# The first load of a streaming logsumexp as two transfers, of the even and of the odd partitions

## The chip, the cores and the metric

The kernel runs on one core of one Trainium2 chip. The metric is the time of the whole execution on the device in microseconds (us). The profile's span is 1.78 to 1.79 us shorter than the time of the same run. The granted clock was 1.0. ACT is ScalarE, DVE is VectorE and SP is SyncE, which here only issues transfers. In the trace of the kernel before each of the 17 loads ends with 16 completions (chunk 0's come at 6.73 to 7.40); they are read here as one for each of the core's 16 DMA engines.

## The reference

```python
def setup_inputs():
    batch, seq, dim = 32, 512, 1024
    return {"x": np.random.randn(batch, seq, dim).astype(np.float32), "axis": -1}

def reference(x, axis):
    x_max = np.max(x, axis=axis, keepdims=True)
    return (x_max.squeeze(axis) + np.log(np.sum(np.exp(x - x_max), axis=axis))).astype(np.float32)
```

There are 16,384 rows of 1,024 floats, 67.1 MB in and 64 KB out. Each of the 128 partitions handles 128 rows.

## The kernel before

The input comes through a ring of 51 rows per partition in 17 loads, all issued by SP. `CHUNKS` lists how many rows a load brings, and how many of them ACT exponentiates in one instruction with the sums left to DVE. The other rows get one ACT instruction each, which also sums.

```python
CHUNKS = [
    (4, 1), (15, 11), (16, 10), (16, 15), (16, 0), (14, 0), (12, 9), (9, 5), (7, 5), (5, 4),
    (4, 3), (3, 0), (2, 2), (2, 2), (1, 0), (1, 0), (1, 0),
]
RING_ROWS = 51
FIRST_PARTS = [("sync", 0, 128)]
# ... (set-up cut)
    def load(i):
        (s, row), r = place[i], CHUNKS[i][0]
        act_wait = max(a for a, _ in busy[s : s + r])
        dve_wait = max(d for _, d in busy[s : s + r])
        if dve_wait:
            nc.sync.wait_ge(dve_done, dve_wait)
        if act_wait:
            nc.sync.wait_ge(act_done, act_wait)
        for engine, lo, hi in FIRST_PARTS if i == 0 else [("sync", 0, P)]:
            getattr(nc, engine).dma_start(
                out=ring[lo:hi, s : s + r], in_=x_v[lo:hi, row : row + r]
            ).then_inc(landed[i], 16)
# ...
    load(0)
    n_early = len(body.instructions)
# ... (the loop over the chunks: load, wait for `landed`, exp, sum)
        nc.scalar.wait_ge(landed[i], 16 * (len(FIRST_PARTS) if i == 0 else 1))
# ... (at the end, the first n_early instructions go ahead of the opening barrier)
```

The load of chunk 0 is issued before the barrier with which the engines start. Everything else comes after it.

The softmax here doesn't subtract the row's maximum and nothing guards it: scores larger than these inputs give would overflow.

## Time and profile before

| | us |
|---|---|
| time, median of 6 runs | 164.12 (164.01 to 164.53) |
| span of the profiled run | 162.2 |
| load stream: first packet, last landing | 1.08, 158.08 |
| landing of chunk 0, of chunk 4 (last of 16 engines) | 7.40, 83.67 |
| DVE, ACT busy | 72.9, 124.1 |

Landings and packet times are read from the trace's semaphore and DMA packet records, which don't name the DMA engine. Below is the timeline of the first us of the kernel before: start, duration, engine, line, operation. "SPq" is SP's sequencer issuing a load.

```profile
0.00 0.37 SPq L85 DMA_DIRECT2D ring<-in_x_dram  x1
...
0.77 1.28 ACT L103 ACT_TABLE_LOAD   x1 [0.77 <-PEq L175]
7.42 1.06 ACT L116 ACTIVATE ring<-ring 128x1024 f32<-128x1024 f32 x1 [5.37 <-DMA ring<-in_x_dram]
```

The first issue takes 0.37 us. ACT's table load starts at 0.77, when a wait for PE's sequencer ends, and SP's next issue follows at 0.78: this is the opening barrier, and the start of the table load marks it. The first exponential waits for chunk 0 until 7.42.

### The profile page before, as it was taken

The page shows a single profiled execution, that of the slowest core. Times are in us where ns is not written, and L with a number is a line of the kernel's source. Part 1 is how long each engine was busy: PE and PEld are TensorE (multiplying, and loading weights), DVE is VectorE, ACT ScalarE, POOL GpSimd, SP SyncE. Part 2 cuts the span into 40 slices and gives each one's busy share as a digit, 9 for nine tenths or more (in the row PEclk, how much of TensorE's full clock was granted, in tenths as well). Part 3 has the DMA queues.
Part 4 walks back from the last instruction along what each step waited for, and adds up shares of the span by engine and source line. Part 5 has one row for each costly group of instructions (what it writes and reads, how often), then busy time and mean ns, then how long its engine had stood idle before and what let it go on. Part 6 is the DMA issues. An engine that isn't in the chain of part 4 may idle for free.

```text
span 162.2 us, 213 instructions
## 1 busy us (share of the span) xinstructions
DVE 72.9 (45%) x11; ACT 124.1 (76%) x136; POOL 0.2 (0%) x4
## 2 busy tenths in 40 slices
DVE  0030000039960799000999900000006999799591
ACT  3180006997099971999339999999999999999993
POOL 0000000000000000000000000000000000000000
DMA  6999899969969959969988999999999999999970
GB/s 263 497 485 470 349 394 517 485 291 517 485 291 517 517 259 517 517 275 501 517 368 370 424 424 432 461 497 388 436 427 399 431 400 439 420 424 414 415 318 16
DMA packets 2593, 67.18 MB, mean 414 GB/s; under 512 B 288, under 2 KB 416, under 8 KB 800
## 3 DMA queue, kind: packets, MB, share of 16 engines
q1 hardware_dynamic: 2448, 67.11, 96.4%
q10 hardware_dynamic: 144, 0.07, 0.1%
q14 instruction: 1, 0.01, 0.0%
HBM read 67.11 MB, written 0.07 MB: 414 GB/s over the span
## 4 chain that ended last, share of the span: by engine, by line
ACT 52%; DMA 38%; DVE 7%; issue 1%
DMA ring<-in_x_dram 38%; ACT ring L128 30%; ACT ring L116 22%; DVE sums L121 7%; ACT res L93 0%
## 5 line engine op out<-in xcount | busy, mean ns | idle before, releaser
L121 DVE TENSOR_REDUCE sums<-ring 128x5 f32<-128x5120 f32 (+8 forms) x11 | 72.9, 6648 | 86.0 <-ACT ring L116 85.9
L116 ACT ACTIVATE ring<-ring 128x5120 f32<-128x5120 f32 (+8 forms) x11 | 59.3, 5394 | 29.4 <-DMA ring<-in_x_dram 29.4
L128 ACT ACTIVATE ring<-ring 128x1024 f32<-128x1024 f32 x61 | 63.4, 1041 | 5.3 <-DMA ring<-in_x_dram 5.3
L128 ACT ACTIVATION_READ_ACCUMULATOR ring<-ring 128x1 f32 x61 | 11.4, 187 | 0.0
L103 ACT ACT_TABLE_LOAD x1 | 1.3, 1283 | 0.8 <-PEq L175 0.8
L93 ACT ACTIVATE res<-sums 128x67 f32<-128x67 f32 (+1 forms) x2 | 0.5, 256 | 0.1
L175 POOL MEMSET const-bfloat16-1.0<- 128x1 bf16 x1 | 0.1, 101 | 0.0
L175 POOL MEMSET const-uint8-127<- 128x1 uint8 x1 | 0.1, 101 | 0.0
L175 POOL MEMSET const-float32-0.0<- 128x1 f32 x1 | 0.1, 98 | 0.2 <-issue 0.2
L175 POOL MEMSET const-float32-1.0<- 128x1 f32 x1 | 0.1, 98 | 0.0
## 6 DMA issues: line engine op xcount, KB each, us to landing
ring<-in_x_dram SPq DMA_DIRECT2D x1, 7680.0 KB, 24.8
ring<-in_x_dram SPq DMA_DIRECT2D x1, 7168.0 KB, 36.1
ring<-in_x_dram SPq DMA_DIRECT2D x1, 6144.0 KB, 21.6
ring<-in_x_dram SPq DMA_DIRECT2D x1, 4608.0 KB, 32.1
ring<-in_x_dram SPq DMA_DIRECT2D x2, 2048.0 KB, 26.3
ring<-in_x_dram SPq DMA_DIRECT2D x1, 3584.0 KB, 40.2
ring<-in_x_dram SPq DMA_DIRECT2D x1, 2560.0 KB, 44.4
ring<-in_x_dram SPq DMA_DIRECT2D x2, 1024.0 KB, 46.0
```

Of the source, the lines that this page charges most:

```text
L93: nc.scalar.activation(out=res[:, lo:hi], in_=sums[:, lo:hi], func=Ln).then_inc(act_done, 1)
L103: nc.scalar.preload_act_table_set("natural_log_exp_and_others")
L116: nc.scalar.activation(out=ring[:, s : s + n_dve], in_=ring[:, s : s + n_dve], func=Exp).then_inc(act_done, 1)
L121: nc.vector.reduce_sum(out=sums[:, row : row + n_dve], in_=ring[:, s : s + n_dve], axis=AX).then_inc(dve_done, 1)
L128: nc.scalar.activation(out=ring[:, s + j], in_=ring[:, s + j], func=Exp, accum_out=sums[:, row + j : row + j + 1],).then_inc(act_done, 1)
L175: nc = _bacc.Bacc("TRN2", target_bir_lowering=False, num_devices=1)
```

## The change

The first load is split in two, presumably so that the DMA engines might get their first work sooner, and by even and odd partitions rather than halves (e2 tries the halves, which cost 3.1%). Both transfers go ahead of the barrier.

```diff
-FIRST_PARTS = [("sync", 0, 128)]
+FIRST_PARTS = [(0, 2), (1, 2)]
...
-        for engine, lo, hi in FIRST_PARTS if i == 0 else [("sync", 0, P)]:
-            getattr(nc, engine).dma_start(
-                out=ring[lo:hi, s : s + r], in_=x_v[lo:hi, row : row + r]
+        for lo, step in FIRST_PARTS if i == 0 else [(0, 1)]:
+            nc.sync.dma_start(
+                out=ring[lo:P:step, s : s + r], in_=x_v[lo:P:step, row : row + r]
             ).then_inc(landed[i], 16)
```

## The prediction

> **What bounds the kernel now.** I read the page first: busy shares (part 1) and the chain that ended last (part 4).
>
> ```profile
> span 162.2 us, 213 instructions
> DVE 72.9 (45%) x11; ACT 124.1 (76%) x136; POOL 0.2 (0%) x4
> ...
> q1 hardware_dynamic: 2448, 67.11, 96.4%
> ...
> ACT 52%; DMA 38%; DVE 7%; issue 1%
> ```
>
> The input moves for 96.4% of the span, while ACT is busy for 76% and DVE for 45%. The load stream is the scarcest resource, although the chain gives 52% to ACT. To see how both fit, I read the chain in order of time:
>
> ```profile
> 0.78 24.82 DMA ring<-in_x_dram
> ...
> 25.62 9.60 ACT ring L116
> ...
> 35.24 11.90 DVE sums L121
> ...
> 47.15 36.52 DMA ring<-in_x_dram
> ...
> 83.69 10.55 ACT ring L128 x21
> ```
>
> Up to 83.67 us the chain is two transfers with a compute step of 21.5 us between them, and that step needs care. The load issued at 47.15 (chunk 4, 16 rows into a reused part of the ring) waits for the first big reduction, so the chain goes through it. But it lands only 36.52 us later, because it queues behind the loads already issued. By the semaphore records chunk 3 has wholly landed at 64.34 and chunk 4 at 83.67: 19.3 us for 8.39 MB, or 434 GB/s. So chunk 4 was issued some 17 us before its turn. The true path is the load stream from its first packet to chunk 4, and the ACT and DVE work before 83.67 has slack. From 83.69 on ACT runs to the end practically without a gap. The waits say the same:
>
> ```profile
> ACT ring L116 <- DMA ring<-in_x_dram: 29.4, 4, 14.0
> ACT ring L128 <- DMA ring<-in_x_dram: 5.3, 1, 5.3
> ```
>
> The last of these ends at 83.69. The load stream itself ends at 158.08 (last landing), 0.1 us before the last exponential starts at 158.19. Both ends of the kernel hang on the stream's start: each us by which the early stream shifts moves the end by about one us.
>
> How the stream starts, from the windows of one us:
>
> ```profile
> 0.00:1.00 1.00, 0.00 (x0) 0.23 (x1) 0.20 (x4) 1.00 0.00 0
> 1.00:2.00 1.00, 0.00 (x0) 1.00 (x1) 0.00 (x0) 1.00 0.92 262
> 2.00:3.00 1.00, 0.00 (x0) 0.06 (x1) 0.00 (x0) 1.00 0.86 360
> 3.00:4.00 1.00, 0.00 (x0) 0.00 (x0) 0.00 (x0) 1.00 1.05 442
> ```
>
> The last column is GB/s: nothing in the first us, then 262 and 360, and the full rate from 3 us on. The packet records give the detail. The first of 128 packets of 16,384 B starts at 1.08 us, 0.70 us after the issue (0.00 to 0.37) ended. The sixteen earliest starts are spread from 1.08 to 1.97. The first packets take 0.61 to 1.36 us, later ones 0.611, which is 16 x 16,384 B / 0.611 us = 429 GB/s. Chunk 0's 16 completions come at 6.73 to 7.40, and that spread of 0.67 us is still there at chunk 4 (83.00 to 83.67). An engine that starts late stays late.
>
> [...]
>
> **The change, part by part.** The listing of the instructions shows one difference: the load of 128x4096 on SP becomes two of 64x4096. ACT, DVE and POOL are the same; ACT's first wait is for 32, not 16.
>
> - Added: one DMA issue on SP ahead of the barrier, between 0.33 and 0.37 us plus a gap of about 0.05. SP reaches the barrier at about 0.95 instead of 0.55, so the barrier opens 0.4 us later. The load of chunk 1 is issued at about 1.2 instead of 0.78. Its first packet is not needed before 6.42, when chunk 0's data of the first engine is through. Cost: 0. ACT's table load (0.77 to 2.06) shifts to about 2.46, while ACT waits for data until 7.42. Cost: 0.
> - Added: 16 completion packets of 9 ns, one per engine. Cost: 0.01 us.
> - Moved: each engine's first share is four packets instead of eight. [...] The total lost at the start is (1 - 262/436) + (1 - 360/436) = 0.57 us of stream, with 436 as the rate from 7.4 to 25.6 us. This caps the gain. Against the halving: the final store, also 128 rows on 16 engines, has its first ten packets within 35 ns[...]. [...] I take about a third of the cap: a gain of 0.2 us.
> - Each engine needs 4 x 0.611 = 2.44 us for its first share, so the second transfer, issued 0.42 us after the first, is ready in time. No gap between them.
>
> Sum: 164.13 - 0.2 + 0.01 = 163.9 us[...].
>
> **The rivals.**
>
> [...] The first 2.1 MB would take 9.8 instead of 4.9 us[...]. Nothing hides this: ACT waits 29.4 us for data early on, and chunk 4 lands later by all of it. The estimate from the packet times is +4 us, 168 us, +2.4%. [...] I give the collision 0.45, and a good part of the full cost in three quarters of such cases.
>
> *Nothing at all.* [...] Then the starts stay spread over 0.9 us and the time is 164.1. For it: even the packets that start last (1.97) need 0.73 us, and all first packets end within 2.05 to 2.69 whatever their start. Against it: the third load's issue takes 0.744 us instead of 0.33, so issuing does press against something at 1.2 to 1.9 us.
>
> *A later barrier costs.* It would add 0.4 us (164.5) if the span's first work depended on it. The windows speak against that: from 2.06 to 7.42 nothing but the load runs.
>
> **Range and chances.** A gain over 2% would need 3.3 us, while at most 0.57 plus part of the 1.08 us is lost before the full rate: 0.01. Without collisions the time is 163.6 to 164.5, within 2%. With them it is 166.5 to 169, with the 2% line at 167.41. Slower by over 2% is 0.45 x 0.75 = 0.34 and I say 0.32. The median of this mixture lies at the top of the first group: 164.1. A range that holds it 8 times in 10 must reach into the second: 163.6 to 168.3.
>
> **What would show each step right or wrong.** Two issues at 0.00 and about 0.42, the barrier 0.4 us later, chunk 1's issue near 1.2: the order of issue. The sixteen first starts: within 0.5 us of the first[...]. The packets of 16,384 B: 0.611 us says no collisions[...]. Chunk 0's last completion: 7.2 in the main case, over 10.5 with collisions, and chunk 4's landing (83.67) must move by as much as chunk 0's, as must the end. If chunk 0 moves and the end doesn't, my claim that the early stream sets the end is wrong. The prediction is also wrong if the later chunks' rates change, for example because the engines' stagger at the start is different.

The main sum came to 163.94 us, given as 163.9: 164.13, less 0.2 for the shorter first share, plus 0.01 for the completions. The 0.2 us is the author's estimate, about a third of the 0.57 us that the windows show lost at the start. "The halving" is that of the spread of the sixteen first starts, 0.89 us, which would have started the last engine 0.45 us earlier; it was an assumption. So was that 64 rows would still use all 16 engines, four packets each. The rival with 9.8 us, later called the collision, is that packets of 64 rows slow each other to half their rate. The 4.9 us is eight packets of 0.611 us; the doubling was assumed. From the 4.9 us added by it, 0.7 to 0.9 us were taken off; +4 us remained.

## The result

The changed kernel takes 164.53 us (median of 6 runs, 164.28 to 164.68), the kernel before 164.12 (6 runs). The ratio is 1.0021, with a 95% interval of 1.0007 to 1.0034: some 0.34 us slower, within 2%. A ratio here is the mean time of one kernel's fast runs over that of the other's in the same rounds, so not quite the ratio of the medians quoted.

The timeline of the changed kernel:

```profile
0.00 0.55 SPq L85 DMA_DIRECT2D ring<-in_x_dram  x1
...
1.84 1.28 ACT L103 ACT_TABLE_LOAD   x1 [1.84 <-PEq L175]
7.59 1.06 ACT L116 ACTIVATE ring<-ring 128x1024 f32<-128x1024 f32 x1 [4.47 <-DMA ring<-in_x_dram]
```

The first issue, now of 64 rows, takes 0.55 us instead of 0.37, and by the records the second takes 0.58. The barrier opens 1.07 us later. Yet chunk 0 is there only 0.17 us later. The windows of one us of the changed kernel (the last column is GB/s):

```profile
core 0: us, DVE busy (x) ACT busy (x) POOL busy (x), PEclk, DMA share, GB/s
1.00:2.00 1.00, 0.00 (x0) 0.16 (x1) 0.00 (x0) 1.00 0.60 164
2.00:3.00 1.00, 0.00 (x0) 1.00 (x1) 0.00 (x0) 1.00 0.88 360
3.00:4.00 1.00, 0.00 (x0) 0.12 (x1) 0.00 (x0) 1.00 0.97 410
```

Where the kernel before moved 262 GB/s in the second us, the changed one moves 164. A window counts a packet's bytes where the packet starts, so the first window shows best that the stream starts later. The chain of the changed kernel:

```profile
1.83 24.25 DMA ring<-in_x_dram
26.09 0.02 issue
26.11 9.60 ACT ring L116
...
35.73 11.90 DVE sums L121
...
47.65 36.51 DMA ring<-in_x_dram
84.15 0.02 issue
84.18 10.56 ACT ring L128 x21
```

It is the chain of before, shifted by 0.5 us from chunk 1 on (26.11 against 25.62, 84.18 against 83.69). The waits for data of the changed kernel say the same:

```profile
ACT ring L116 <- DMA ring<-in_x_dram: 28.8, 4, 14.3
ACT ring L128 <- DMA ring<-in_x_dram: 5.3, 1, 5.3
```

ACT waits 0.6 us less in total at L116. It has been held 1.07 us longer by the barrier and then waits 0.9 us less for chunk 0 (4.47 against 5.37). Less waiting is no gain here: the wait before chunk 1 grew from 14.0 to 14.3.

What matters at the start can be read from three packet figures: when the first packet starts, when the sixteen earliest-starting packets have ended on average, and when the 16 engines have finished chunk 0 on average.

| trace | first issue | first packet starts | first 16 packets end, mean | chunk 0 landed, mean / last | chunk 4 landed, last |
|---|---|---|---|---|---|
| before | 0.37 | 1.08 | 2.40 | 7.07 / 7.40 | 83.67 |
| changed | 0.55 | 1.34 | 2.70 | 7.33 / 7.57 | 84.15 |

### The profile page after: what moved, and what is told of

It reads as the page before. It is cut to its first block, busy times and chain, and to the rows that moved or that the text cites. A ratio compares the mean times of both kernels' runs of the same rounds, so it can differ in the third digit from the quotient of the medians.

```text
span 162.7 us, 214 instructions
## 1 busy us (share of the span) xinstructions
DVE 72.9 (45%) x11; ACT 124.1 (76%) x136; POOL 0.2 (0%) x4
## 4 chain that ended last, share of the span: by engine, by line
ACT 52%; DMA 37%; DVE 7%; issue 1%
DMA ring<-in_x_dram 37%; ACT ring L128 30%; ACT ring L116 22%; DVE sums L121 7%; ACT res L93 0%
## 5 line engine op out<-in xcount | busy, mean ns | idle before, releaser
L116 ACT ACTIVATE ring<-ring 128x5120 f32<-128x5120 f32 (+8 forms) x11 | 59.3, 5394 | 28.8 <-DMA ring<-in_x_dram 28.8
```

What stands on the lines that cost most here:

```text
L116: nc.scalar.activation(out=ring[:, s : s + n_dve], in_=ring[:, s : s + n_dve], func=Exp).then_inc(act_done, 1)
```

## The experiments

**Theory A**: the 64-row shape makes the first issue longer, hence the first packet later, and the end follows. **Rival B**: the later barrier and the later issue of chunk 1 cost. **Rival C**: a second issue in the queue slows the first. What two halves cost comes on top (e2). The experiments share one loop:

```diff
-        for lo, step in FIRST_PARTS if i == 0 else [(0, 1)]:
-            nc.sync.dma_start(
-                out=ring[lo:P:step, s : s + r], in_=x_v[lo:P:step, row : row + r]
+        for engine, lo, hi, step, a, b in FIRST_PARTS if i == 0 else [("sync", 0, P, 1, 0, r)]:
+            getattr(nc, engine).dma_start(
+                out=ring[lo:hi:step, s + a : s + b], in_=x_v[lo:hi:step, row + a : row + b]
```

A part is thus (engine, first partition, end, step, first row, end row), and each experiment differs from the changed kernel in `FIRST_PARTS`, unless more is shown. All results were correct. The times in the last but one column are those of the profiled execution. The runs were made in three groups on different chips (e1 to e4; e5 to e8 and e12; e9 to e11). The kernel before had a median of 164.01 us in the first and 164.32 to 164.33 in the others, so the ratio, taken within a group, is what can be compared, and an expected time in us only to some 0.3 us.

| run | first issue | first packet | chunk 0, mean / last | chunk 4, last | that run's time | ratio to before (95%) |
|---|---|---|---|---|---|---|
| e1 rows2 | 0.36 | 1.00 | 6.92 / 7.13 | 83.43 | 163.87 | 1.0010 (0.9996 to 1.0024) |
| e2 halves | 0.55 | 1.33 | 12.07 / 12.36 | 88.44 | 169.24 | 1.0310 (1.0297 to 1.0324) |
| e3 odd late | 0.54 | 1.32 | 7.88 / 9.15 | 85.37 | 165.62 | 1.0089 (1.0076 to 1.0103) |
| e4 two queues | 0.55 | 1.34 | 13.58 / 14.49 | 84.61 | 164.97 | 1.0029 (1.0012 to 1.0045) |
| e5 late | 0.36 | 1.72 | 7.75 / 8.24 | 84.49 | 164.80 | 1.0045 (1.0032 to 1.0058) |
| e6 quarters | 0.54 | 1.33 | 7.70 / 8.13 | 84.49 | 164.95 | 1.0048 (1.0035 to 1.0060) |
| e7 odd first | 0.55 | 1.41 | 7.31 / 7.50 | 84.08 | 164.75 | 1.0022 (1.0009 to 1.0034) |
| e8 rows 1 + 3 | 0.37 | 1.00 | 6.93 / 7.24 | 83.84 | 164.44 | 1.0002 (0.9989 to 1.0016) |
| e9 mixed | 0.36 | 0.99 | 7.06 / 7.36 | 83.79 | 164.31 | 1.0008 (0.9994 to 1.0021) |
| e10 rows2, two queues | 0.37 | 1.00 | 13.95 / 14.30 | 83.80 | 164.17 | 0.9994 (0.9981 to 1.0008) |
| e11 rows2 again | 0.37 | 1.00 | 7.06 / 7.42 | 84.01 | 164.29 | 0.9998 (0.9983 to 1.0012) |
| e12 before again | 0.37 | 1.01 | 7.14 / 7.44 | 83.98 | 164.27 | 1.0009 (0.9995 to 1.0023) |

In all these traces and those of before and after, the time less chunk 4's last landing is 80.25 to 80.80 us. It is 80.25 to 80.46 except in e2, e7, e8 and e9, where the next chunk came so late that ACT waited 0.17 to 0.44 us for it. The end hangs on the stream in every one.

The ratios fall into two groups. Six runs issue a first load of 128 partitions ahead of the barrier (e1, e8 to e12, e12 being the kernel before against itself): 0.9994 to 1.0010. Six issue one of fewer partitions there (the changed kernel, e2, e3, e4, e6, e7): 1.0021 and more. Between single runs of the two groups the intervals can overlap.

### e1: two transfers by rows, of all 128 partitions

```diff
-FIRST_PARTS = [(0, 2), (1, 2)]
+FIRST_PARTS = [("sync", 0, 128, 1, 0, 2), ("sync", 0, 128, 1, 2, 4)]
```

> Two transfers ahead of the barrier, but each of all 128 partitions and two of the four rows (packets of 8,192 B). Theory A (the shape of 64 rows makes the issue slow, 0.55 us instead of 0.37, and so the first packet late): the first issue takes 0.37 us again, the first packet starts at 1.08, and the end is 164.1 to 164.2. Rival B (what costs is that there are two transfers ahead of the barrier: the barrier opens about 1 us later and chunk 1 is issued later): first packet at 1.08, yet the end is 164.4 to 164.6 as in the changed kernel. Rival C (a second issue slows the first one, whatever its shape): first issue 0.55 us, first packet 1.34.

The timeline of this kernel:

```profile
0.00 0.36 SPq L85 DMA_DIRECT2D ring<-in_x_dram  x1
```

With 128 rows the issue takes 0.36 us although a second follows, so C falls. The first packet is at 1.00. The barrier lets ACT go at 1.24, and chunk 1 is issued then, 0.46 us later than in the kernel before. The median of 164.3 lies between A's figure and B's. The ratio of 1.0010 has an interval from nothing to the full cost, so it doesn't decide between A and B. The repeat e11 gave 0.9998 and leaves B little room.

### e2: two halves

```diff
-FIRST_PARTS = [(0, 2), (1, 2)]
+FIRST_PARTS = [("sync", 0, 64, 1, 0, 4), ("sync", 64, 128, 1, 0, 4)]
```

> Two transfers of 64 partitions each, but partitions 0 to 63 and 64 to 127 (step 1). Theory A1 (64 rows are slow to issue): first issue 0.55 us as with even and odd. Theory A2 (the step of two partitions is slow to issue): first issue 0.37 us. [...]packets of 16,384 B take about 1.2 us instead of 0.611, chunk 0 lands 4 to 5 us later than 7.4, and the time is 168 to 169. [...]

The figures from the 1.2 us on are those for halves loaded at half the rate, an assumption; 1.2 us is about twice 0.611. If halves cost nothing, 164.1 to 164.6 was expected.

The windows of this kernel:

```profile
3.00:4.00 1.00, 0.00 (x0) 0.11 (x1) 0.00 (x0) 1.00 1.12 229
4.00:5.00 1.00, 0.00 (x0) 0.00 (x0) 0.00 (x0) 1.00 0.72 147
5.00:6.00 1.00, 0.00 (x0) 0.00 (x0) 0.00 (x0) 1.00 1.09 229
```

The stream runs at about half its rate (147 to 246 GB/s in the windows from 3 to 10 us, against 410 to 426 in the changed kernel's from 3 to 6), and most packets after the first two of a share take 1.26 to 1.29 us instead of 0.611. What in the chip halves the rate was not shown. Chunk 0 lands 4.96 us after the kernel before's and the end is 3.1% later, 5.1 us (a median of 169.14, just above the 168 to 169 expected): a loss at the very start passes to the end whole. With even and odd partitions (changed, e7) the median packet takes 0.611 us and 109 or 110 of the 128 at most 0.63, so nothing of this happens there. The first issue takes 0.55 us at a step of 1 too (A1): the number of rows (64, against 0.37 us with 128), not the step, makes it long.

### e3: the odd partitions behind the barrier

```diff
-FIRST_PARTS = [(0, 2), (1, 2)]
+FIRST_PARTS = [("sync", 0, 128, 2, 0, 4), ("sync", 1, 128, 2, 0, 4)]
...
-    n_early = len(body.instructions)
+    n_early = 1
```

> As changed, but only the even partitions are loaded ahead of the barrier and the odd ones behind it. Theory A: the first packet still starts at 1.34 (the issue of 64 even rows is slow by itself), and the end is 164.4 to 164.6, although the barrier opens 0.6 us earlier than in the changed kernel. Rival B (the late barrier costs): the end is back at 164.1 to 164.3. Rival C (a second issue in the queue slows the first): first issue 0.37 us.

The first issue and two windows of this kernel:

```profile
0.00 0.54 SPq L85 DMA_DIRECT2D ring<-in_x_dram  x1
...
4.00:5.00 1.00, 0.00 (x0) 0.00 (x0) 0.00 (x0) 1.00 0.79 295
5.00:6.00 1.00, 0.00 (x0) 0.00 (x0) 0.00 (x0) 1.00 0.99 393
```

The first packet starts at 1.32 and the first issue takes 0.54 us, although no second issue follows ahead of the barrier: as A has it and C doesn't. But the end was expected at 164.4 to 164.6 and came at 165.52, a miss. The odd transfer was issued at 1.18 and its issue ended at 1.66, yet between 4.5 and 5.5 only 12 to 14 of the 16 engines have a packet in flight. Some engines had presumably used up their even share and had no odd packet yet. The packets are longer too: an engine's eight of chunk 0 take 5.67 us on average, against 5.18 in the changed kernel, which is most of the 0.55 us by which chunk 0's mean landing is later. One engine ends chunk 0 at 9.15 when the mean is 7.88. Its packets, each starting where the one before ended, can be followed from there to chunk 4, where it is still 1.1 us behind the mean (85.37 against 84.27). So the split seems to put at risk that the second part is there in time. In the changed kernel, with the second issue at 0.605, at least 15 of the engines had a packet from 3 us on. Why some engines got the odd rows so late, and why the packets were longer, is open.

### e4: the odd partitions through ACT's queue

```diff
-FIRST_PARTS = [(0, 2), (1, 2)]
+FIRST_PARTS = [("sync", 0, 128, 2, 0, 4), ("scalar", 1, 128, 2, 0, 4)]
```

> Even partitions issued by SP, odd ones by ACT, both ahead of the barrier. Theory A: SP's issue still takes 0.55 us and the first packet starts at about 1.34, the barrier at about 0.9; the end is 164.3 to 164.6. Rival B: with the barrier only some 0.2 us late the end is 164.1 to 164.2.

ACT issued the odd part at 0.12 us, and it landed only at 14.49. The engines took packets of the two queues in turn (by the packet records, one of the odd part about every 2.9 us on each engine once chunk 1 was under way), so it shared them with chunk 1. That does no harm by itself: the first exponential came late, but ACT had slack until chunk 1 (14.0 us of waiting before it in the kernel before). The cost of 0.29% can't be told from the changed kernel's 0.21%. SP's issue of 0.55 us and the first packet at 1.34 are as A has them (ACT's issue of 64 rows took 0.55 us too, that of 128 rows in e10 0.38); the barrier opened at 1.47, not at the expected 0.9, so the run says little about B. In this trace more was lost in chunks 2 to 4, where packets of 65,536 B took 2.45 us on average instead of 2.42.

### e5: one load, but behind the barrier

```diff
-FIRST_PARTS = [(0, 2), (1, 2)]
+FIRST_PARTS = [("sync", 0, 128, 1, 0, 4)]
...
-    n_early = len(body.instructions)
+    n_early = 0
```

> The kernel before with its one first load moved behind the opening barrier, nothing else. It delays the stream's first packet without touching a shape. Theory A (the end follows the stream's start one to one): the first packet starts 0.4 to 0.8 us later against the first load's issue in the kernel before, and the whole time rises by the same 0.4 to 0.8 us, to 164.5 to 164.9. Rival (the slack of ACT and DVE hides a late start): 164.0 to 164.2.

The timeline of this kernel:

```profile
0.73 1.28 ACT L103 ACT_TABLE_LOAD   x1 [0.73 <-PEq L175]
0.73 0.36 SPq L85 DMA_DIRECT2D ring<-in_x_dram  x1
```

The barrier is earlier here than in the kernel before and no shape has changed; only the issue is at 0.73 instead of 0.00. The first packet starts 0.64 us later, chunk 0 lands 0.68 us later on average, and the time rises by 0.45%, 0.74 us. That is one to one within the interval (0.53 to 0.95 us). The median of 165.03 is above the 164.5 to 164.9 expected, in a group in which the kernel before took 164.32.

### e6: four quarters

```diff
-FIRST_PARTS = [(0, 2), (1, 2)]
+FIRST_PARTS = [("sync", k, 128, 4, 0, 4) for k in range(4)]
```

(The kernel that ran had the four parts written out.)

> Four transfers of every fourth partition (32 rows each), all ahead of the barrier. If an issue takes longer the fewer rows a transfer has, the first issue takes over 0.55 us, the first packet starts later than 1.34 and the end is 164.7 or more. If any shape but 128 rows costs the same 0.55, the first packet starts at 1.34 again, and four issues of 0.55 open the barrier at about 2.9 us; the end stays at 164.4 to 164.6 if the late barrier costs nothing. Each engine's share of a transfer is then two packets (1.22 us) and an issue every 0.6 us keeps ahead of it. Packets stay at 0.611.

The timeline of this kernel:

```profile
0.00 0.54 SPq L85 DMA_DIRECT2D ring<-in_x_dram  x1
```

An issue of 32 rows takes 0.54 us and the first packet is at 1.33: both as with 64. So the cost of the first issue doesn't grow as rows fall; every shape here short of 128 partitions has it. But the end at 165.02 is a miss: 164.4 to 164.6 was expected with these figures, some 0.2 us more in this group. The four parts landed on average at 3.74, 5.01, 6.43 and 7.70, steps of 1.27, 1.42 and 1.27 us, where two packets of 0.611 are 1.22 us. Chunk 0 was thus 0.37 us later than in the changed kernel. The packet records take this apart: an engine's eight packets take 5.45 us on average against 5.18, so 0.27 us is longer packets, and 0.10 us is time without a packet. From 2.1 to 2.85 us only 10 to 14 of the 16 engines have one in flight; in the changed kernel at least 15 do from 2.3 us on. Why is open.

### e7: the odd partitions first

```diff
-FIRST_PARTS = [(0, 2), (1, 2)]
+FIRST_PARTS = [("sync", 1, 128, 2, 0, 4), ("sync", 0, 128, 2, 0, 4)]
```

> The changed kernel with the odd partitions first. A repeat in all that the theories name: first issue 0.55, first packet 1.34, end 164.3 to 164.7. It shows whether chunk 1's long packets (seven of its first sixteen took 2.48 to 2.85 us instead of 2.27 in the changed kernel) come back (systematic) or not (chance): if they are part of the cost, chunk 1's last landing is again 0.5 us after the kernel before's 25.6, otherwise 0.2 to 0.3.

The same result: 1.0022, issue 0.55, chunk 0 at 7.31 on average against 7.33. The long packets at the start of chunk 1 came back, but weaker: five of the first sixteen at 2.35 to 2.71 us, against seven (2.34 to 2.85) in the changed kernel. Among chunk 1's first sixteen packets, those over 2.3 us number nine in e3 and all sixteen in e2, but none in the three traces with one load (before, e5, e12). They aren't tied to the shape alone: e4 has none there, e9 and e11 two each, and in other places such packets turn up too, in e6 at 16 us and in e8 and e12 at 20. Chunk 1 landed 0.32 us after the first trace of before, near what was expected if they are chance, so whether they belong to the change stays open.

### e8: one row, then three

```diff
-FIRST_PARTS = [(0, 2), (1, 2)]
+FIRST_PARTS = [("sync", 0, 128, 1, 0, 1), ("sync", 0, 128, 1, 1, 4)]
```

> Two transfers of all 128 partitions: one row each first (packets of 4,096 B), then three rows (12,288 B). If smaller first packets let the sixteen engines start closer together, as two rows each did (spread 0.53 instead of 0.89 us), the spread is below 0.5 us and chunk 1 lands 0.2 to 0.3 us before the kernel before's 25.6; the end 163.7 to 164.0. Rival[...]: 164.1 to 164.5.

The rival's reasons were that the small packets' own cost eats the gain (4,096 B take a median of 0.161 us, where a quarter of 0.611 is 0.153) or that the second transfer isn't ready in time.

The sixteen earliest packets started within 0.34 us, but three of them had ended by then, so they can be those of fewer than sixteen engines. Sixteen packets are in flight at once only 0.42 us after the first start; that is below 0.5 us too, as hoped. Chunk 0 landed 0.13 us earlier on average. But seven packets at 20 us took up to 2.81 us, chunk 1's last landing was 25.79, and the time is unchanged (1.0002): the end of 163.7 to 164.0 didn't come, and the rival's 164.1 to 164.5 did. Taken as the time until sixteen packets are in flight, the start's spread goes with the first packets' size where one queue is used: 0.42 us with 4,096 B, 0.49 to 0.53 with 8,192 (e1, e9, e11), 0.76 to 0.92 with 16,384 (before, changed, e2, e3, e5, e7, e12), whether the transfer has 128 rows or 64. Two runs don't fit: four quarters (e6) take 1.75 us and e10, with 8,192 B through two queues, 0.98. The reason was not tested.

### e9: two rows of all partitions, then even and odd

```diff
-FIRST_PARTS = [(0, 2), (1, 2)]
+FIRST_PARTS = [("sync", 0, 128, 1, 0, 2), ("sync", 0, 128, 2, 2, 4), ("sync", 1, 128, 2, 2, 4)]
```

> First load in three transfers ahead of the barrier: rows 0 and 1 of all 128 partitions, then rows 2 and 3 of the even and of the odd partitions. The two 64-row transfers and a barrier later than in the changed kernel (at about 2.2 us) are kept; only the very first transfer has 128 rows again. Theory A (the late first packet is what costs): first packet at 1.00, as with two rows each, end within 0.15 us of the kernel before. Rival B (the late barrier and the late issue of chunk 1) and rival D (64-row transfers anywhere ahead of the barrier cost, for instance by gaps between an engine's shares): 0.3 to 0.8 us over the kernel before.

The timeline of this kernel:

```profile
0.00 0.36 SPq L85 DMA_DIRECT2D ring<-in_x_dram  x1
...
2.24 1.28 ACT L103 ACT_TABLE_LOAD   x1 [2.24 <-PEq L175]
```

The barrier is 0.4 us later than even in the changed kernel, and both 64-row transfers are there. But the first packet is at 0.99 and chunk 0 lands at 7.06 on average, as in the kernel before. The cost is 0.08%, 0.13 us, with an interval from -0.1 to 0.34 us. A is favoured, as its figure is met; the lowest figure of B, and of D (64-row transfers anywhere ahead of the barrier cost), 0.3, lies just inside the interval. The kernel before against itself gave 1.0009 (e12), so 1.0008 can't be told from nothing. The landing of chunk 0 is the stronger evidence.

### e10: by rows, through two queues

```diff
-FIRST_PARTS = [(0, 2), (1, 2)]
+FIRST_PARTS = [("sync", 0, 128, 1, 0, 2), ("scalar", 0, 128, 1, 2, 4)]
```

> Rows 0 and 1 of all partitions issued by SP, rows 2 and 3 by ACT. If the extra 0.6 us of even on SP and odd on ACT came from the 64-row shape (late first packet), this ends with the kernel before or below (164.0 to 164.3 where that has 164.1). If it came from two queues taking turns on the engines, it costs 0.3 us or more again, and the part issued by ACT lands later than 10 us.

Both expectations met in part: ACT's part lands at 14.30, so the queues do take turns, but it costs nothing (0.9994). The two queues were not what made e4 slow.

### e11 and e12: repeats

> A repeat of two transfers of 128 partitions and two rows each, to see whether its profile (chunk 4 landed 0.24 us earlier than in the kernel before) or its first timing (ratio 1.001, 0.9996 to 1.0024) is what holds. Theory A gives 0 to 0.2 us below the kernel before; if the first packet's 0.08 us is eaten by chance stretches later, no difference.

> The kernel before once more, to see how much of two traces' difference is chance. First issue 0.37 us, first packet at 1.08, ratio 1.000. In the traces so far the last landing of chunk 4 minus the start of the first packet lies between 82.4 and 84.0 us (81.8 to 83.1 for halves and odd_late without their extra cost); if it differs from the first trace's 82.60 by 0.2 us or so, then the 0.2 us that the changed kernel lost beyond its later first packet is within chance.

e11 is the kernel of e1 once more, e12 the kernel before. The second trace of two rows each has chunk 4 at 84.01, the first 83.43. The second trace of the kernel before has it at 83.98, the first 83.67: 82.97 us after its first packet against 82.60. Two executions of one kernel thus differ by 0.3 to 0.6 us at chunk 4 by chance; long packets (two over 2.3 us at the start of chunk 1 in e11, some at 20 us in e12) may be much of it. The start varies less. Chunk 0's mean landing was 7.07 and 7.14 in the two traces of before, 7.33 and 7.31 in those of even and odd, though 6.92 and 7.06 in those of two rows each. No version tried beats the kernel before by more than its noise.

## Why the prediction was right or wrong

**What bounds the kernel: right.** The early stream sets the end, us for us. The later start in e5 and the slower first 2.1 MB in e2 came out at the end whole (0.64 to 0.68 us gave 0.74; 4.96 us gave 5.1).

**The later barrier costs nothing: right in its conclusion, wrong in its size.** The barrier came 1.07 us later rather than 0.4. The issues took 0.55 and 0.58 us rather than 0.33 to 0.37; the barrier then opened 0.65 us after the end of the second issue, where before it opened 0.40 us after the end of the first; why is open. Chunk 1's issue moved to 1.83 instead of 1.2. e9, with a still later barrier, loses 0.13 us by the best estimate, not resolved from zero.

**"Added: one DMA issue on SP": the step that failed.** It counted the new issue and took the first issue's duration from a row with 128 partitions. The first issue itself got longer, 0.55 instead of 0.37, and nothing hides that one: the first packet starts only 0.71 us after its end before, and 0.79 us after it now. The first packet came later by 0.33 us (mean of 1.34 and 1.41 against mean of 1.08 and 1.01), and chunk 0 landed 0.22 us later on average (mean of 7.33 and 7.31 against mean of 7.07 and 7.14). This 0.22 us is the part of the 0.34 us that the runs show. In the same pairs of traces chunk 1 and chunk 4 land 0.32 us later on average; the 0.1 us between is about what the longer packets of chunk 1 add (a mean of 2.290 and 2.281 us against 2.269 and 2.274, eight to an engine). Whether they belong to the change is open (e7), and 0.1 us is inside the interval (0.11 to 0.56 us) and inside what two traces of one kernel differ by.

**"Moved: each engine's first share is four packets instead of eight": failed too.** The gain of 0.2 us didn't come. The sixteen starts were spread over 0.92 us (1.34 to 2.27) instead of halving. The working assumed that the spread goes with the number of rows; the reason it gave was not shown. With one queue the spread goes with the packet's size (0.42 us at 4,096 B, 0.76 to 0.92 at 16,384 B) and is the same with 128 rows as with 64 (e8); what sets it is open. That 64 rows use all 16 engines, as the prediction assumed, held: each of the two parts brought 16 landings spread over 0.5 us, and 16 packets were in flight at once.

**Collisions: the rival didn't happen.** The packets of 16,384 B kept to a median of 0.611 us. That packets of 64 rows can slow to about half their rate shows in e2 (1.26 to 1.29 us), where it cost 5.1 us, though not why; the estimate of 4 us for a doubling was in the right region. The chance of 0.45 given to it is what stretched the range up to 168.3.

**The number: inside the range, partly by luck.** The measured 164.53 lies inside 163.6 to 168.3, just above the group without collisions (163.6 to 164.5). The median of 164.1 equals the figure of "nothing at all" only because it is the middle of a mixture with collisions. The main sum of 163.9 had the sign wrong. The nearest figure is the 164.5 of "a later barrier costs", and that is chance: it stood for 0.4 us from the barrier, which the runs don't support, while the longer first issue is in none of the rivals.

## What to carry to other kernels

When the load stream sets the end from its first byte, the first issue is on the critical path, while the later ones here had slack as long as they came in time (e9, with chunk 1 issued behind a barrier at 2.24, has a ratio of 1.0008; e3's odd part was late, 1.0089): keep the first transfer at the full 128 partitions (a first issue at 0.00 took 0.36 to 0.37 us and the first packet started at 0.99 to 1.08, against 0.54 to 0.55 and 1.32 to 1.41 with 64 or 32), and split along rows if at all (0.9994 to 1.0010). Partition halves can halve the rate (e2: most packets at 1.26 to 1.29 us, 3.1% in all) where even and odd partitions don't (a median of 0.611). Before explaining a few tenths of a us by a second trace, take a second trace of the same kernel.
